# A two-layer encoder on one core: gate and up weight combinations built by accumulating DMAs, with other signs in the seven-product scheme

## The chip, the cores and the metric

One NeuronCore of a Trainium2 chip runs the whole program in one launch. The metric is the device time of that launch in microseconds (us). The engines are TensorE (PE, with its weight loads shown apart as PEld), VectorE (DVE), ScalarE (ACT), GpSimd (POOL) and SyncE (SP), which here only issues DMAs. Each engine works through its own queue in order and waits on semaphores of the others.

## The reference, cut to what matters

Two layers run over 768 tokens (512 of one request and 256 of another) with 1024 features. Each layer is a mixer (differential attention and a two-direction mLSTM), a layer norm, a feed-forward part and a second layer norm. All arithmetic is in float32. The change touches the feed-forward part and the step into it:

```python
def _conv_ffn(x, w_gu, conv_w, conv_b, w_down):
    gu = x @ w_gu                          # 1024 -> 2 * 2816
    gate, up = gu[..., :D_FF], gu[..., D_FF:]
    conv = conv_b + sum(gp[:, j:j + S] * conv_w[j] for j in range(3))   # gp: gate, padded
    hmid = jax.nn.gelu(conv) * up
    return hmid @ w_down
```

## The kernel before

**Precision.** Every matrix product is made of three passes: each float32 operand is split into a rounded part (`wh`, made by ACT) and the rest (`wl`, made by DVE), and PE adds up high by high, high by low and low by high. The splitting of one weight block of 128x512 is called a conversion here: an ACT activation (L172) and a DVE subtraction (L173).

**The gate and up products.** For each of the 22 blocks `f` of 128 hidden features, gate and up (2 outputs), the two halves of the 1024 input features and the two halves of the tokens form a two by two by two product. `ff_tile` does it with seven products of half size in the place of eight (Strassen's scheme in Winograd's form). It needs four combinations of activations (S1 to S4), made once a layer in `combine`, transposed and split in `to_strassen`, and four combinations of weights per `f`: with g0, g1 the two halves of the gate weights and u0, u1 those of the up weights, t1 = u0 - g0, t2 = u1 - t1, t3 = u1 - u0, t4 = t2 - g1. Each product is 12 matmuls of 128x384. Six PSUM banks are handed out in turn to the products (`FTAGS`).

**The weights' way.** `Weights` holds a list of pieces (DMAs of 128x512 float32, 256 KB, issued by SP into six `raw` buffers), and a list of blocks in the order in which PE takes them. Up to `NSLOT` = 12 converted blocks are held ahead of PE: when a block has been used (`done`), `pump` converts the next. A block that is a combination is built in `_value` (L150) from raw pieces just ahead of its conversion: t1 and t3 on POOL, t2 and t4 on DVE, each into one buffer of its own (tags T1 to T4). The blocks of one `f` stand in the order g0, g1, t4, t2, t3, t1, u1; for the first two (`FF_EARLY`) g0 and g1 come earlier and their first two products run ahead. The pool for the combinations (`diff_pool`) is opened in each layer at the start of the stage `wo`, in which the mixer's output projection, the residual and the first layer norm are computed in two halves of six token tiles (L881, L884, `half_stats`, `layer_norm`).

**Around it.** In the second half of `wo` each token tile goes through DVE (residual, statistics, norm), POOL (the power in `layer_norm`, L829 and L830, and `combine` for tiles 3 and 4) and then through PE transposes and ACT and DVE splits (`transposed_split`, L363 to L366). `todo` lists the five results of a tile in the order A22, S2, S3, S1, S4. The products in `ff_tile` run in the order A11, A12, A22 (p4), S2 (p6), S3 (p7), S1 (p5), S4 (p3). What DVE does with them ends in `g` (the gate, L941 and L950) and `up` (L954, L957); then come the convolution over tokens (ACT L958, DVE L960 and L961), gelu (L962), the product with up (L963) and the split of the result (L967, L968). `down(gi)` multiplies three or four such blocks with the down weights (L985, 128x512 matmuls) and adds them to the residual (L990, L992); it stands one `f` behind the group that it uses, except after the last group of a layer. The framework orders each engine's queue when the program is built, by the priorities that `prio` sets and by what it reckons to be ready.

Of the kernel before, what the change touches and what calls it, by code (L numbers as in the profile page):

```python
# [86 lines left out]
NSG = 3  # L87
AT1 = 11
# [8 lines left out]
class Weights:  # L97
# [3 lines left out]
    def __init__(self, nc, raw_pool, hl_pool, prio):  # L101
# [3 lines left out]
        self.n_dma = self.n_conv = self.n_got = self.n_done = 0  # L105
# [10 lines left out]
    def block(self, src, n, dst=None):  # L116
        self.blocks.append((src, n, dst))
        for j in self._pieces(src):
            self.uses[j] += 1
# [5 lines left out]

    def _pieces(self, src):

        if not isinstance(src, dict):
            return [src]
        if src.get("planned"):  # L130
            return []
        src["planned"] = True
        return self._pieces(src["a"]) + self._pieces(src["b"])


    def _load(self):

        while self.n_dma < len(self.dram) and (self.n_dma < NRAW or self.uses[self.n_dma - NRAW] == 0):
# [4 lines left out]
            self.n_dma += 1  # L143

    def _value(self, src, n):
        if isinstance(src, dict):
            if "tile" not in src:
                a, b = self._value(src["a"], n), self._value(src["b"], n)
                src["tile"] = self.diff_pool.tile([128, 512], F32, tag=src["tag"], name=f"{src['tag']}_{self.n_conv}")
                src["engine"].tensor_tensor(out=src["tile"], in0=a, in1=b, op=ALU.subtract)  # L150
                for x in (src["a"], src["b"]):
                    if not isinstance(x, dict):
                        self.uses[x] -= 1
            return src["tile"]
        return self.raw[src]

    def _conv(self, i):
# [16 lines left out]
        if not isinstance(src, dict):  # L174
            self.uses[src] -= 1
        self._load()

    def pump(self):

        live = sum(1 for j in range(self.n_done, self.n_conv) if self.blocks[j][2] is None)  # L180
        while self.n_conv < len(self.blocks):
            if isinstance(self.blocks[self.n_conv][0], dict) and self.diff_pool is None:
                break
# [23 lines left out]
def trunk(ctx, nc, tc, d, o, depth=DEPTH):  # L207
# [59 lines left out]
    for l in range(depth):  # L267
# [19 lines left out]
        for kind, i in ffn_seq:  # L287
            if kind == "f":

                def half(w, p):  # L290
                    return W.piece(d[w][l, i, :, p * 512:(p + 1) * 512], 512)

                if i in early:
                    g0, g1 = early[i]
                else:
                    g0, g1 = half("w_g", 0), None
                u0, u1 = half("w_u", 0), half("w_u", 1)
                if g1 is None:
                    g1 = half("w_g", 1)
                t1 = {"a": u0, "b": g0, "tag": "T1", "engine": G}  # L300
                t2 = {"a": u1, "b": t1, "tag": "T2", "engine": V}
                t3 = {"a": u1, "b": u0, "tag": "T3", "engine": G}
                t4 = {"a": t2, "b": g1, "tag": "T4", "engine": V}
                for src in (t4, t2, t3, t1, u1) if i in early else (g0, g1, t4, t2, t3, t1, u1):
                    W.block(src, 512)
# [63 lines left out]
    for l in range(depth):  # L369
# [431 lines left out]
        DF = ExitStack()  # L801
        W.diff_pool = df = DF.enter_context(tc.tile_pool(name=f"df{l}", bufs=1, reuse_waits="tile"))
# [51 lines left out]
        def combine(t):  # L854
# [73 lines left out]
        def ff_tile(f):  # L928
# [173 lines left out]
```

## Time and profile before

| | us |
|---|---|
| runs shown | 1831.13, 1832.51, 1832.93 (median 1832.51) |
| profiled execution, device time | 1831.93 |
| its span | 1830.1 |
| PE busy in the span | 1796.4 (98%) |
| DVE busy | 1345.2 (74%) |
| ACT busy | 768.2 (42%) |
| POOL busy | 241.8 (13%) |

The profile shows one execution. The span is the time from its first to its last recorded instruction; 1.8 us of the device time lie around it. The page gives busy times by engine; other views give the same by stretch of time, by line of the kernel, by wait, and as a chain of work followed back from the last instruction. A PE matmul is pipelined: one of 128x384 is shown as about 0.34 us, though one can start every 0.17 us, so the distance between starts is the time that a product costs. TensorE's granted clock is 0.999 of full speed over the span.

### The profile page before, as it was taken

How to read it: one execution, taken by the hardware profiler on the slowest of the kernel's cores; microseconds unless marked ns; L12 is line 12 of the kernel's file. 1: busy time of each engine (PE TensorE's matmuls, PEld its weight loads, DVE VectorE, ACT ScalarE, POOL GpSimd, SP SyncE). 2: the span in 40 equal slices, each digit the busy share in tenths (PEclk: the TensorE clock that was granted, in tenths of full speed). 3: DMA queues.
4: the chain of work that ended last, by engine and by line, in shares of the span. 5: the costliest groups of instructions: out<-in, count | busy, mean ns of one | idle time of the engine just before them, and what ended most of it. 6: DMA issues, size and time to landing. Idle time of an engine off the chain costs nothing.

```text
span 1830.1 us, 26254 instructions
## 1 busy us (share of the span) xinstructions
PE 1796.4 (98%) x9692; PEld 1580.8 (86%) x9692; DVE 1345.2 (74%) x2576; ACT 768.2 (42%) x1624; POOL 241.8 (13%) x260
## 2 busy tenths in 40 slices
PE   8999999999999999999999999999999999999998
PEld 8877777889899899899898777778898898898996
DVE  5546777589887787787955467785998787777878
ACT  4445567235334343243233556671443343343340
POOL 2001001141111111110110011011411111111102
PEclk9999999999999999999999999999999999999999
DMA  5312110402222122122232112113031221221211
GB/s 188 100 52 70 53 47 29 168 3 89 82 81 75 53 72 74 62 64 94 99 96 80 53 63 69 31 55 141 24 98 54 81 81 47 81 81 47 81 64 69
DMA packets 83280, 134.95 MB, mean 74 GB/s; under 512 B 7984, under 2 KB 27056, under 8 KB 83152
## 3 DMA queue, kind: packets, MB, share of 16 engines
q1 hardware_dynamic: 82432, 132.90, 22.8%
q8 instruction: 76, 1.25, 0.3%
q14 instruction: 52, 0.43, 0.1%
q10 hardware_dynamic: 720, 0.37, 0.1%
HBM read 126.86 MB, written 6.39 MB: 73 GB/s over the span
## 4 chain that ended last, share of the span: by engine, by line
PE 81%; DVE 11%; ACT 2%; POOL 2%; issue 2%; DMA 1%; SPq 0%; DVEq 0%; POOLq 0%; ACTq 0%
PE p L925 32%; PE dn L985 16%; PE wo L881 5%; PE aqkA L356 4%; PE av L346 3%; PE lo L346 3%; PE lv L346 3%; PE aqkB L356 2%; DVE wl L173 2%; PE u L727 2%; PE c1a L346 2%; PE c1b L346 2%; PE num L621 1%; PE num L617 1%; PE s L711 1%
## 5 line engine op out<-in xcount | busy, mean ns | idle before, releaser
L925 PE MATMUL p<-actA,wh 128*128 128x384 f32 x1408 | 363.4, 338 | 3.2 <-DVE g L950 3.2
L172 ACT ACTIVATE wh<-raw 128x512 fp32r<-128x512 f32 (+1 forms) x348 | 214.8, 629 | 287.5 <-PE p L925 109.1
L173 DVE TENSOR_TENSOR wl<-raw,wh 128x512 fp32r<-128x512 f32 (+1 forms) x348 | 243.4, 710 | 64.9 <-ACT wh L172 64.5
L925 PE MATMUL p<-actB,wh 128*128 128x384 f32 x1056 | 270.1, 337 | 0.0
L925 PEld LDWEIGHTS p<-actA,wh 128*128 128x128 f32 x1408 | 254.7, 188 | 5.8 <-DVE g L950 3.9
L925 PE MATMUL p<-actA,wl 128*128 128x384 f32 x704 | 237.3, 337 | 0.0
L150 POOL TENSOR_TENSOR T<-raw,raw 128x512 f32<-128x512 f32 x88 | 119.8, 1364 | 837.4 <-DVE wl L173 504.9
L985 PE MATMUL dn<-wh,actB 128*128 128x512 f32 x576 | 208.8, 396 | 1.4 <-DVE acc L992 1.4
L172 ACT ACTIVATE wh<-T 128x512 fp32r<-128x512 f32 x176 | 108.2, 628 | 220.0 <-DVE acc L992 104.9
L925 PEld LDWEIGHTS p<-actB,wh 128*128 128x128 f32 x1056 | 191.3, 188 | 0.0
L985 PE MATMUL dn<-wh,ring 128*128 128x512 f32 x480 | 179.2, 397 | 1.6 <-DVE acc L992 1.6
L925 PE MATMUL p<-actB,wl 128*128 128x384 f32 x528 | 177.2, 336 | 0.0
L992 DVE TENSOR_TENSOR acc<-acc,dn 128x512 f32<-128x512 f32 x144 | 98.2, 682 | 71.9 <-PE dn L985 71.6
L173 DVE TENSOR_TENSOR wl<-T,wh 128x512 fp32r<-128x512 f32 x176 | 129.4, 747 | 22.4 <-ACT wh L172 22.2
L985 PEld LDWEIGHTS dn<-wh,actB 128*128 128x128 f32 x576 | 108.0, 188 | 29.7 <-DVE acc L992 3.5
L925 PEld LDWEIGHTS p<-actA,wl 128*128 128x128 f32 x704 | 132.2, 188 | 0.1
L881 PE MATMUL wo<-wh,actB 128*128 128x512 f32 x384 | 122.9, 397 | 0.0
L985 PE MATMUL dn<-wl,actB 128*128 128x512 f32 x288 | 113.2, 393 | 0.0
L985 PEld LDWEIGHTS dn<-wh,ring 128*128 128x128 f32 x480 | 90.0, 188 | 24.7 <-DVE acc L992 4.2
L925 PEld LDWEIGHTS p<-actB,wl 128*128 128x128 f32 x528 | 99.1, 188 | 0.0
L985 PE MATMUL dn<-wl,ring 128*128 128x512 f32 x240 | 94.5, 394 | 0.0
L881 PEld LDWEIGHTS wo<-wh,actB 128*128 128x128 f32 x384 | 71.8, 188 | 16.2
(265 smaller groups left out, 3390.0 us busy)
## 6 DMA issues: line engine op xcount, KB each, us to landing
raw<-in_w_g_dram SPq DMA_DIRECT2D x88, 256.0 KB, 2.6
raw<-in_w_u_dram SPq DMA_DIRECT2D x88, 256.0 KB, 2.8
raw<-in_w_down_dram SPq DMA_DIRECT2D x88, 256.0 KB, 2.9
raw<-in_w_out_dram SPq DMA_DIRECT2D x32, 256.0 KB, 2.6
pt<-scr_m SPq DMA_DIRECT2D x12, 512.0 KB, 4.2
raw<-in_w_c_dram SPq DMA_DIRECT2D x16, 264.0 KB, 3.6
raw<-in_w_av_dram SPq DMA_DIRECT2D x16, 256.0 KB, 4.3
raw<-in_w_aq_dram SPq DMA_DIRECT2D x16, 256.0 KB, 3.7
```

Source lines behind the costliest of these rows:

```text
L150: src["engine"].tensor_tensor(out=src["tile"], in0=a, in1=b, op=ALU.subtract)
L172: self.nc.scalar.activation(h, v, AF.Identity)
L173: self.nc.vector.tensor_tensor(out=l, in0=v, in1=h.bitcast(F32), op=ALU.subtract)
L346: PE.matmul(ps, xh(k, t, a), (h, l)[b][:, cols], start=k + i == 0, stop=k == 7 and i == 2)
L356: PE.matmul(ps, w, actA[:, k, b, tok], start=n == 0, stop=n == 23)
L617: PE.matmul(pn[:, di * 256:di * 256 + 129], qet[r, di, hh // 2, :], cst[di, c][r, hh // 2, :], start=di == dirs[0], stop=False, skip_group ...
L621: PE.matmul(pn[:, di * 256:di * 256 + 129], pt[:, di, hh, :], vaug[:, c, hh, :], start=not dirs and di == 0, stop=di == 1, skip_group_chec ...
L727: PE.matmul(pu[:, qt * 128:(qt + 1) * 128], aT[:, st * 128:(st + 1) * 128], av[:, s0 + st, h * 128:(h + 1) * 128], start=st == 0, stop=st ...
L881: PE.matmul(p, actB[:, k, a, t * 128:(t + 1) * 128], units[k][1 + b], start=n + i == 0, stop=n == 7 and i == 2)
L925: PE.matmul(ps, blk[1 + a][:, k * 128:(k + 1) * 128], x[:, k, b, :], start=k + i == 0, stop=k == 3 and i == 2)
L985: PE.matmul(p, x, (wh_, wl_)[b], start=k + i == 0, stop=k == nf - 1 and i == 2)
L992: V.tensor_tensor(out=z, in0=z, in1=p, op=ALU.add)
```

## The change

The four weight combinations of each `f` are no longer computed by POOL and DVE. For each, SP loads a base piece from HBM into a buffer of a ring of four (`NSUM`, tag T), and POOL issues a second DMA into the same buffer that adds its source to what is there: t1 = u0 + g0, t2 = u1 + t1, t3 = u1 + u0, t4 = g1 + t2, where t1 and t2 as addends are read from their buffers in SBUF. The signs of the scheme are changed so that weights are only added: `combine` builds other signs for S1, S2 and S4 with the same number of instructions, and `ff_tile` has as many DVE operations as before. A sum is issued when its layer has begun and the sum four places earlier has been converted. The blocks of one `f` now stand in the order g0, g1, t1, t2, t3, t4, u1, and the products run in the order A11, A12, S1 (p5), S2 (p6), S3 (p7), A22 (p4), S4 (p3). u0 is no longer a raw piece, and g0 and g1 are read by DMA again for the sums.

```diff
@@ class Weights
     def block(self, src, n, dst=None):
         self.blocks.append((src, n, dst))
-        for j in self._pieces(src):
-            self.uses[j] += 1
+        if not isinstance(src, dict):
+            self.uses[src] += 1
+
+    def sum(self, base, plus):
+        s = {"base": base, "plus": plus, "read": False}
+        self.sums.append(s)
+        return s
@@ def _load(self):
+        while self.diff_pool is not None and self.n_sum < len(self.sums) and (self.n_sum < NSUM or self.sums[self.n_sum - NSUM]["read"]):
+            s = self.sums[self.n_sum]
+            if s["layer"] != self.layer:
+                break
+            s["tile"] = t = self.diff_pool.tile([128, 512], F32, tag="T", name=f"T{self.n_sum}", bufs=NSUM)
+            self.nc.sync.dma_start(t, s["base"])
+            plus = s["plus"]
+            self.nc.gpsimd.dma_start(t, plus["tile"] if isinstance(plus, dict) else plus, accum_op=ALU.add)
+            self.n_sum += 1
@@ def _value(self, src, n):
-            if "tile" not in src:
-                a, b = self._value(src["a"], n), self._value(src["b"], n)
-                src["tile"] = self.diff_pool.tile([128, 512], F32, tag=src["tag"], name=f"{src['tag']}_{self.n_conv}")
-                src["engine"].tensor_tensor(out=src["tile"], in0=a, in1=b, op=ALU.subtract)
...
@@ def trunk (the order of the blocks)
-                t1 = {"a": u0, "b": g0, "tag": "T1", "engine": G}
-                t2 = {"a": u1, "b": t1, "tag": "T2", "engine": V}
-                t3 = {"a": u1, "b": u0, "tag": "T3", "engine": G}
-                t4 = {"a": t2, "b": g1, "tag": "T4", "engine": V}
-                for src in (t4, t2, t3, t1, u1) if i in early else (g0, g1, t4, t2, t3, t1, u1):
+                u1 = W.piece(at("w_u", 1), 512)
+                t1 = W.sum(at("w_u", 0), at("w_g", 0))
+                t2 = W.sum(at("w_u", 1), t1)
+                t3 = W.sum(at("w_u", 1), at("w_u", 0))
+                t4 = W.sum(at("w_g", 1), t2)
...
+                for src in (t1, t2, t3, t4, u1) if i in early else (g0, g1, t1, t2, t3, t4, u1):
@@ def combine(t):
-            E.tensor_tensor(out=s1, in0=y0, in1=y1, op=ALU.add)
-            E.tensor_tensor(out=s2, in0=s1, in1=x0, op=ALU.subtract)
+            E.tensor_tensor(out=s1, in0=y1, in1=y0, op=ALU.subtract)
+            E.tensor_tensor(out=s2, in0=s1, in1=x0, op=ALU.add)
             E.tensor_tensor(out=s3, in0=x0, in1=y0, op=ALU.subtract)
-            E.tensor_tensor(out=s4, in0=x1, in1=s2, op=ALU.subtract)
+            E.tensor_tensor(out=s4, in0=s2, in1=x1, op=ALU.subtract)
@@ def ff_tile(f):
             V.tensor_tensor(out=g[:, lo_], in0=p2, in1=m1, op=ALU.add)
-            p4 = bank(f"p4_{f}")
-            product(p4, A22)
+            p5 = bank(f"p5_{f}")
+            product(p5, S1)
             p6 = bank(f"p6_{f}")
             product(p6, S2)
-            V.tensor_tensor(out=u2, in0=p6, in1=m1, op=ALU.add)
+            V.tensor_tensor(out=u2, in0=m1, in1=p6, op=ALU.subtract)
+            V.tensor_tensor(out=u4, in0=p5, in1=u2, op=ALU.add)
             p7 = bank(f"p7_{f}")
             product(p7, S3)
             V.tensor_tensor(out=u3, in0=p7, in1=u2, op=ALU.add)
-            V.scalar_tensor_tensor(out=g[:, hi_], in0=p4, scalar=-1.0, in1=u3, op0=ALU.mult, op1=ALU.add)
-            p5 = bank(f"p5_{f}")
-            product(p5, S1)
-            V.tensor_tensor(out=u4, in0=p5, in1=u2, op=ALU.add)
-            V.tensor_tensor(out=up[:, hi_], in0=p5, in1=u3, op=ALU.add)
+            V.scalar_tensor_tensor(out=up[:, hi_], in0=p5, scalar=-1.0, in1=u3, op0=ALU.mult, op1=ALU.subtract)
+            p4 = bank(f"p4_{f}")
+            product(p4, A22)
+            V.tensor_tensor(out=g[:, hi_], in0=p4, in1=u3, op=ALU.add)
             p3 = bank(f"p3_{f}")
             product(p3, S4)
-            V.tensor_tensor(out=up[:, lo_], in0=p3, in1=u4, op=ALU.add)
+            V.scalar_tensor_tensor(out=up[:, lo_], in0=p3, scalar=-1.0, in1=u4, op0=ALU.mult, op1=ALU.subtract)
```

## Rows read from the trace of the kernel before

**Rows 1.** The page, part 1: busy us (share) xinstructions by engine.
```profile
PE 1796.4 (98%) x9692; PEld 1580.8 (86%) x9692; DVE 1345.2 (74%) x2576; ACT 768.2 (42%) x1624; POOL 241.8 (13%) x260
```

**Rows 2.** Busy time by stretch: us, each engine's busy time (instructions), clock, DMA share, GB/s.
```profile
core 0: us, PE busy (x) PEld busy (x) DVE busy (x) ACT busy (x) POOL busy (x), PEclk, DMA share, GB/s
...
375.00:426.00 51.00, 48.63 (x276) 43.08 (x276) 47.14 (x69) 19.34 (x35) 20.88 (x20) 1.00 0.11 37
426.00:480.00 54.00, 54.00 (x283) 50.01 (x282) 51.64 (x87) 26.94 (x45) 8.56 (x6) 1.00 0.27 85
480.00:880.00 400.00, 398.40 (x2086) 371.27 (x2086) 306.97 (x501) 151.23 (x246) 42.76 (x32) 1.00 0.24 74
...
1284.00:1335.00 51.00, 48.69 (x276) 43.05 (x275) 47.12 (x69) 19.27 (x34) 20.91 (x20) 1.00 0.12 37
...
1390.00:1790.00 400.00, 398.61 (x2086) 371.52 (x2085) 305.86 (x500) 149.04 (x242) 42.43 (x32) 1.00 0.21 68
```

**Rows 3.** What PE waited for, whole span: us in total, times, longest.
```profile
PE p L925 <- DVE g L950: 3.2, 2, 1.6
PE dn L985 <- DVE acc L992: 3.0, 10, 0.5
```

**Rows 4.** The chain that ended last, 487 to 560 us: start, us, what.
```profile
487.13 43.97 PE p L925 x252
...
538.45 0.60 DVE T L150
539.05 0.61 DVE acc L992
539.66 0.04 issue
539.70 16.86 PE dn L985 x72
556.56 3.50 PE p L925 x20
```

**Rows 5.** Groups by line: the building of the combinations (busy us, mean ns, idle before).
```profile
L150 POOL TENSOR_TENSOR T<-raw,raw 128x512 f32<-128x512 f32 x88 | 119.8, 1364 | 837.4 <-DVE wl L173 504.9 <-DMA raw<-in_w_u_dram 194.0 <-DVE g L950 86.9
L150 DVE TENSOR_TENSOR T<-raw,T 128x512 f32<-128x512 f32 x44 | 32.2, 731 | 18.2 <-POOL T L150 18.2
L150 DVE TENSOR_TENSOR T<-T,raw 128x512 f32<-128x512 f32 x44 | 30.0, 682 | 0.1
```

**Rows 6.** Timeline of PE, 408 to 424 us: start, us, what, [idle before].
```profile
408.42 0.60 PE L925 MATMUL p<-actA,wh 128*128 128x384 f32 x2
...
411.39 0.52 PE L925 MATMUL p<-actB,wh 128*128 128x384 f32 x2
...
422.27 0.61 PE L925 MATMUL p<-actA,wh 128*128 128x384 f32 x2 [1.62 <-DVE g L950]
```

**Rows 7.** Timeline of DVE, 408 to 422 us.
```profile
408.60 1.87 DVE L366 TENSOR_TENSOR actB<-y0T,actB 128x512 fp32r<-128x512 f32 x3
...
411.59 0.68 DVE L150 TENSOR_TENSOR T<-raw,T 128x512 f32<-128x512 f32 x1
...
416.72 4.10 DVE L173 TENSOR_TENSOR wl<-raw,wh 128x512 fp32r<-128x512 f32 x3
420.75 0.54 DVE L949 TENSOR_TENSOR u<-p,u 128x384 f32<-128x384 f32 x1
```

**Rows 8.** Timeline of POOL in the stage wo of the first layer.
```profile
357.75 2.82 POOL L150 TENSOR_TENSOR T<-raw,raw 128x512 f32<-128x512 f32 x2 [34.47 <-DVE acc L884]
363.62 1.28 POOL L829 TENSOR_SCALAR rsa<-mva 128x1 f32<-128x1 f32 x1 [3.06 <-DVE mva L828]
...
398.45 0.19 POOL L829 TENSOR_SCALAR rsa<-mva 128x1 f32<-128x1 f32 x1
```

**Rows 9.** Timeline of all engines at the last block of the first layer.
```profile
876.58 0.55 DVE L950 SCALAR_TENSOR_TENSOR g<-p,u 128x384 f32<-128x384 f32 x1
...
882.38 0.95 DVE L963 TENSOR_TENSOR up<-up,c 128x768 f32<-128x768 f32 x1
...
884.54 0.30 PEld L985 LDWEIGHTS dn<-wh,actB 128*128 128x128 f32 x2 [0.27 <-DVE actB L968]
```

**Rows 10.** The page, part 6: DMA issues, KB each, median us to landing.
```profile
raw<-in_w_u_dram SPq DMA_DIRECT2D x88, 256.0 KB, 2.8
...
acc<-in_x_dram SPq DMA_DIRECT2D x6, 512.0 KB, 6.3
...
lng<-in_ln_g_dram SPq DMA_DIRECT2D x4, 512.0 KB, 8.6
```

More of the change, by code (lines that the diff above doesn't have):

```diff
@@ L87 @@
 NSG = 3
+NSUM = 4
 AT1 = 11
@@ L104, in __init__ @@
         self.uses, self.raw, self.hl = {}, {}, {}
-        self.n_dma = self.n_conv = self.n_got = self.n_done = 0
+        self.n_dma = self.n_conv = self.n_got = self.n_done = self.n_sum = 0
+        self.sums = []
         self.diff_pool = None
@@ L124, in unit @@
             self.block(self.piece(ap[:, c], n // 2), n // 2)
[L126 to L133, printed above, removed]
     def _load(self):
@@ L143, in _load @@
             self.n_dma += 1
+        while self.diff_pool is not None and self.n_sum < len(self.sums) and (self.n_sum < NSUM or self.sums[self.n_sum - NSUM]["read"]):
[7 more added lines that the diff above has]
+            self.n_sum += 1
     def _value(self, src, n):
         if isinstance(src, dict):
-            if "tile" not in src:
-                a, b = self._value(src["a"], n), self._value(src["b"], n)
-                src["tile"] = self.diff_pool.tile([128, 512], F32, tag=src["tag"], name=f"{src['tag']}_{self.n_conv}")
-                src["engine"].tensor_tensor(out=src["tile"], in0=a, in1=b, op=ALU.subtract)
-                for x in (src["a"], src["b"]):
-                    if not isinstance(x, dict):
-                        self.uses[x] -= 1
             return src["tile"]
@@ L173, in _conv @@
         self.nc.vector.tensor_tensor(out=l, in0=v, in1=h.bitcast(F32), op=ALU.subtract)
-        if not isinstance(src, dict):
+        if isinstance(src, dict):
+            src["read"] = True
+        else:
             self.uses[src] -= 1
@@ L181, in pump @@
         while self.n_conv < len(self.blocks):
-            if isinstance(self.blocks[self.n_conv][0], dict) and self.diff_pool is None:
-                break
+            if isinstance(self.blocks[self.n_conv][0], dict):
+                self._load()
+                if "tile" not in self.blocks[self.n_conv][0]:
+                    break
             if self.blocks[self.n_conv][2] is None:
@@ L288, in trunk, with at @@
             if kind == "f":
[L290 to L299, printed above, removed]
-                t1 = {"a": u0, "b": g0, "tag": "T1", "engine": G}
-                t2 = {"a": u1, "b": t1, "tag": "T2", "engine": V}
-                t3 = {"a": u1, "b": u0, "tag": "T3", "engine": G}
-                t4 = {"a": t2, "b": g1, "tag": "T4", "engine": V}
-                for src in (t4, t2, t3, t1, u1) if i in early else (g0, g1, t4, t2, t3, t1, u1):
+                def at(w, p):
+                    return d[w][l, i, :, p * 512:(p + 1) * 512]
+                g0, g1 = early[i] if i in early else [W.piece(at("w_g", p), 512) for p in range(2)]
+                u1 = W.piece(at("w_u", 1), 512)
[3 more added lines that the diff above has]
+                t4 = W.sum(at("w_g", 1), t2)
+                for t_ in (t1, t2, t3, t4):
+                    t_["layer"] = l
+                for src in (t1, t2, t3, t4, u1) if i in early else (g0, g1, t1, t2, t3, t4, u1):
                     W.block(src, 512)
@@ L801, in trunk @@
         DF = ExitStack()
+        W.layer = l
         W.diff_pool = df = DF.enter_context(tc.tile_pool(name=f"df{l}", bufs=1, reuse_waits="tile"))
```

## The prediction

> **What bounds the kernel now.** I read the busy times first. PE is busy for 98% of the span, DVE for 74%, POOL for 13% [rows 1]. The reader should see that the engines which the change relieves are not the one that is full. Since an average hides stages, the second view is busy time by stretch. In the two long feed-forward stretches PE works 398.4 and 398.6 of 400 us, while DVE works about 306 and POOL about 42 [rows 2]. The steps into the feed-forward part are looser: PE misses 2.4 us of 51 in the first layer and 2.3 in the second, and there DVE works 47 of 51 [rows 2]. The third view is the chain of waits, for what a feed-forward round costs: 252 matmuls of the gate and up products take 43.97 us, 0.1745 each, so a product of 12 takes 2.09 us; a round of three blocks f (487.13 to 556.56, the start of the next chain of products) takes 69.4 us, 23.1 per f [rows 4]. The fourth is the list of PE's waits: within the feed-forward part only two kinds are worth a name, a bank held until `g` is written (3.2 us in two waits, one per layer) and a bank of the down products held until DVE has added it to the residual (3.0 us in ten waits) [rows 3].
>
> From these, a ceiling for any gain: PE idle in the four kinds of stretch that the change touches is 2.4 + 2.3 (the steps) + 1.6 + 1.4 (the long stretches) = 7.7 us [rows 2]. That is 0.4% of the time, and part of it is due to transposes and splits that stay.
>
> **Work removed.** 88 POOL operations of 1364 ns and 88 DVE operations of about 707 ns go, 119.8 and 62.2 us [rows 5]. Almost all of it lies beside full PE work, so it is worth nothing by itself. It is on the path at two places. In a round, one DVE sum of 0.60 us stands in the chain directly before the addition that frees a bank for the down products [rows 4]; the ten such waits make 3.0 us [rows 3], and without the sum I take two thirds of it away: -2.0 us (bounds 0 and -3.0). At the step into the feed-forward part, the two DVE sums of the second f (the first at 411.59) and the conversions behind them, the last ones 4.1 us long, stand in DVE's queue ahead of u2 at 420.75, which `g` and then PE's wait of 1.62 us hang on [rows 6, 7]. Two sums are 1.2 us of DVE's time by the 0.60 that one costs in a chain [rows 4]. But the second f's sums can start only when the first f's buffers have been converted, so the conversions may come later in turn. I take half: -0.6 a layer, -1.2 in all (bounds 0 and -3.2, the whole of the waits).
>
> **The accumulating DMAs.** No row shows a DMA issued by POOL or one that adds. Per f there are four base loads on SP and four adding DMAs on POOL, in place of one load less (u0) and with g0 and g1 still loaded raw: 11 transfers of 256 KB instead of 4, besides the two of the down weights. That is (11 + 2) x 0.262 MB per 23.1 us, 147 GB/s, where the stretch now moves 74 at a DMA share of 0.24 [rows 2]; the share doubles and stays under half, so I cost bandwidth at nothing. What counts is the latency L of one adding DMA, from issue to landing. A plain load of this size lands after 2.8 us; loads of twice the size after 6.3 and 8.6 [rows 10]. These are the bounds; an adding DMA reads two sources of 256 KB, which puts it nearest to the 6.3, and I take 5 to 6. POOL's queue is in order: t2 waits for t1 to land, t3 is issued behind t2, t4 waits for t2, and the next t1 stands behind t4. So a round of four costs POOL two latencies plus four issues; at the 1.3 us that an operation of POOL costs here [rows 8] that is 2L + 5.2 = 17 us of the 23.1. Up to 12 blocks are converted ahead, which is 25 us of products at 2.09, so a late sum is covered. Price taken: 0. Nothing else is queued on POOL in the feed-forward part until the last group's layer norm, when all sums of the layer are long done.
>
> **Moved past in the stage wo.** The first four sums go out where POOL now builds two of the first f (357.75), and the norm of the first tile uses POOL at 363.62 [rows 8]. If t2 or t4 stands ahead of it, the norm waits for up to one L. That delays one DVE operation and its successors, while the output projection has three banks and each tile takes some 24 matmuls; I take 0. The next sums come when POOL still has the norm of the last tile to serve (398.45) [rows 8]; if an adding DMA waits there ahead of it for its base load, that is up to 2.8 us a layer [rows 10] straight on DVE's full queue. Price taken 0, bounds 0 and +5.6 for both layers.
>
> **The order of the products.** The transposed results of the last tile still come in the order A22, S2, S3, S1, S4, but the first product now needs S1 instead of A22. Today the product on A22 runs before 411.39, where the one on S2 starts [rows 6], while DVE is still splitting the last three results for actB, of which S1 is the last, until 410.47 [rows 7]. With S1 first, PE has no product for that time; it starts on S1 at about 410.5, 0.9 us earlier than it starts on S2 now, but still owes A22's 2.09: +1.2 us a layer, +2.4 in all. Bounds: 0, if the framework lets A22's product go first when it sees S1 late, and +2.1 a layer.
>
> At the end of a layer the gate's second half `g` is now written after the sixth product instead of the fifth, 2.09 us of PE later. The last f of a layer has no other f behind it, and there the chain g (876.58), convolution, gelu, product with up (882.38), split is already late by 0.27 us for PE's down products at 884.54 [rows 9]. Today u3 and a conversion stand between the fifth product's end and `g`, each about 0.6 us of DVE (as in rows of its kind, 0.54 [rows 7] and 0.60 [rows 4]); in the new order they are done before the sixth product ends, so about 1.2 of the 2.09 is made good and +0.9 a layer shows, +1.8 in all (bounds 0 and +4.2). Elsewhere a block's result is used a whole f later, at no cost. The other edits (signs in `combine`, `ff_tile`, the ring of four buffers in place of four single ones) keep the number and the shapes of the instructions: 0.
>
> **The sum.** -2.0 - 1.2 + 2.4 + 1.8 = +1.0 us on the profiled 1831.9, so 1832.9. The profiled execution lies 0.6 under the median of the runs shown: 1833.5.
>
> **A rule that speaks against the change.** In the feed-forward stretch DVE is busy for 307 of 400 us [rows 2], and POOL's two-input operations there take 1364 ns in the mean [rows 5]. The Trainium skill, "SBUF — State Buffer", section "SBUF: two separate sides", says that a DMA issued from GpSimd has its descriptors written by GpSimd's cores through a port pair that VectorE can lock them out of, so that such a DMA can take several times as long beside VectorE work. It also says that this belongs to VectorE's two-port modes, and infers that an operation of two tensors does not stop descriptors. No run so far shows either. By the rule L would grow by the wait for DVE, which is the second rival below, and I give it a small share of that chance. The same skill, "DMA: Bandwidth & Descriptors", section "Anatomy of one DMA", fits 2.0 us plus bytes over 436 GB/s, 2.6 us for 256 KB; with that L the sum stays as it is.
>
> **Rivals.** (1) DVE's relief counts in full and the new order costs nothing: -3.0 - 3.2 = -6.2, 1826. For it: both waits are DVE's, and DVE loses 62 us. Against it: S1 is the last of the three splits. Chance 0.20. (2) The sums starve PE, slower: the place is POOL's queue, the mechanism the chain t1, t2, t4 with a wait for landing twice per f, and it decides from 2L + 5.2 = 23.1, L = 9.0 us; beyond it each f costs 2(L - 9.0), so at L = 10 the 44 of them cost 88 us, 1920. For it: nothing in the trace bounds an adding DMA, and 8.6 us occurs for a transfer [rows 10]. Against it: that row has twice the bytes and a queue before it. Chance 0.08. (3) The bubbles at the two ends of the feed-forward part come at their upper bounds: 2 x (2.1 + 2.1) = 8.4, less the 2.0 of the rounds, +6.4 and 1839; an adding DMA ahead of the norm on POOL gives about as much. Chance 0.22.
>
> **Chances and range.** The forecast has 0.50. A measurement of this kernel can tell about 0.2%, 3.7 us, from no change. Faster by more: 0.19, nearly all of rival 1. Slower by more: rivals 2 and 3 and a little of the forecast, 0.33. Within: 0.48. The forecast's own range is 1829 to 1837; the range given reaches to rival 1 and beyond rival 3 with one late norm, 1825 to 1845, and leaves rival 2 out.
>
> **What would show it.** Right: PE busy stays above 398 of 400 in the long stretches; PE's wait for the residual's addition shrinks below 3.0 us; a wait of PE for a split of actB appears at the first product of each layer's feed-forward part; POOL's issues are spaced well under 23 us per four. Wrong: ACT or DVE conversions waiting for the adding DMAs for tens of us in total with PE idle behind them (rival 2), or no new wait at the step and a shorter one for `g` (rival 1).

## The result, and the profile after

The changed kernel takes 1847.08 us (median; 1846.36 to 1849.45) beside 1832.61 for the kernel before on the same chip: 1.0085 times, interval 1.0073 to 1.0098. It is slower by 14.5 us, where 1833.5 was forecast with a range up to 1845. The profiled execution after is the slowest of its four, 1849.45 us with a span of 1847.7, beside a span of 1830.1 before, so the traces have 17.6 us to explain.

The page of the changed kernel, parts 1 and 6 (busy time by engine; DMA issues with KB each and median us to landing):

```profile
PE 1801.1 (97%) x9692; PEld 1587.1 (86%) x9692; DVE 1257.9 (68%) x2488; ACT 771.2 (42%) x1624; POOL 274.5 (15%) x348
...
T<-in_w_u_dram SPq DMA_DIRECT2D x132, 256.0 KB, 3.6
...
T<-T POOLq DMA_DIRECT2D x88, 256.0 KB, 4.3
...
T<-in_w_g_dram POOLq DMA_DIRECT2D x44, 256.0 KB, 4.9
T<-in_w_u_dram POOLq DMA_DIRECT2D x44, 256.0 KB, 5.7
```

DVE has lost 87 us against [rows 1] and PE does the same 9692 matmuls. An adding DMA lands after 4.3 to 5.7 us, against 2.8 for a plain load before [rows 10].

The same stretches as in [rows 2], changed kernel (us, busy time of PE, PEld, DVE, ACT and POOL, clock, DMA share, GB/s):

```profile
375.00:426.00 51.00, 45.67 (x256) 39.20 (x254) 40.38 (x61) 19.37 (x35) 20.48 (x22) 1.00 0.33 81
426.00:480.00 54.00, 49.60 (x259) 46.91 (x260) 43.11 (x79) 25.86 (x42) 11.37 (x14) 0.97 0.76 182
480.00:880.00 400.00, 400.00 (x2090) 373.02 (x2089) 276.10 (x468) 150.14 (x244) 57.33 (x66) 1.00 0.60 148
1284.00:1335.00 51.00, 48.03 (x265) 40.83 (x265) 40.51 (x58) 16.39 (x30) 21.03 (x22) 1.00 0.21 49
1335.00:1390.00 55.00, 48.63 (x252) 47.67 (x251) 41.69 (x75) 26.48 (x45) 10.65 (x12) 0.91 0.78 191
1390.00:1790.00 400.00, 400.00 (x2078) 371.10 (x2077) 275.79 (x466) 148.58 (x241) 60.24 (x68) 1.00 0.60 147
```

The two long stretches got better: PE is busy for all of 400 us where it missed 1.6 and 1.4. The whole loss lies in the 100 us around the start of each feed-forward part. There PE is idle for 5.3 + 4.4 us in the first layer (2.4 + 0 before [rows 2]) and for 3.0 + 6.4 in the second (2.3 + 0 before), and the clock falls to 0.97 and 0.91 in the mean. The stretch from 1335 that [rows 2] leaves out, in the kernel before:

```profile
1335.00:1390.00 55.00, 55.00 (x288) 51.11 (x288) 52.13 (x89) 27.00 (x45) 8.65 (x6) 1.00 0.28 87
```

What PE waited for, whole span, changed kernel (us in total, times, longest):

```profile
PE p L929 <- DVE up L955: 12.9, 4, 4.0
...
PE y1T L366 <- DVE actA L369: 2.8, 2, 2.2
...
PE y0T L366 <- DVE actA L369: 1.9, 2, 1.4
...
PE dn L989 <- DVE acc L994: 0.9, 1, 0.9
```

The two kinds of wait in [rows 3] are gone (the wait for `g`) or down from 3.0 to 0.9 (the down products). A new kind stands in their place, four waits of 12.9 us in all: a PSUM bank held until DVE has written the second half of `up` (L955). All four fall in the start of a feed-forward part. Here they are in the timeline of PE (start, us, what, idle before):

```profile
426.84 0.62 PE L929 MATMUL p<-actB,wh 128*128 128x384 f32 x2 [3.99 <-DVE up L955]
...
459.00 0.62 PE L929 MATMUL p<-actA,wh 128*128 128x384 f32 x2 [2.52 <-DVE up L955]
...
1343.42 1.01 PE L929 MATMUL p<-actB,wh 128*128 128x384 f32 x2 [3.88 <-DVE up L955]
...
1376.12 0.66 PE L929 MATMUL p<-actA,wh 128*128 128x384 f32 x2 [2.49 <-DVE up L955]
```

**Why `up` is late.** Timelines of POOL, ACT and DVE ahead of the first of these waits, changed kernel (`wh` is ACT's half of a conversion, `wl` DVE's, and T is a buffer of the ring):

```profile
419.33 0.88 POOL L150 DMA_DIRECT2D T<-in_w_g_dram  x1 [2.20 <-ACT wh L173]
...
403.41 0.64 ACT L173 ACTIVATE wh<-T 128x512 fp32r<-128x512 f32 x1 [2.79 <-DMA T<-in_w_g_dram]
...
424.96 0.63 ACT L173 ACTIVATE wh<-T 128x512 fp32r<-128x512 f32 x1 [2.43 <-DMA T<-in_w_g_dram]
...
413.87 1.28 DVE L174 TENSOR_TENSOR wl<-T,wh 128x512 fp32r<-128x512 f32 x2
...
418.71 0.69 DVE L174 TENSOR_TENSOR wl<-T,wh 128x512 fp32r<-128x512 f32 x1 [3.09 <-ACT wh L173]
...
423.42 0.55 DVE L954 TENSOR_TENSOR u<-p,u 128x384 f32<-128x384 f32 x1
425.62 0.69 DVE L174 TENSOR_TENSOR wl<-T,wh 128x512 fp32r<-128x512 f32 x1 [1.65 <-ACT wh L173]
426.23 0.55 DVE L955 SCALAR_TENSOR_TENSOR up<-p,u 128x384 f32<-128x384 f32 x1
```

Read it from the end. `up` at 426.23 needs only p5 and the u3 that DVE wrote at 423.42; it could have run at about 424. But DVE's queue is in order, and ahead of `up` stands the conversion of the first sum of the third f, at 425.62. That waits for ACT's half of the conversion at 424.96, which has waited 2.43 us for the adding DMA. POOL issued that DMA at 419.33 into the ring buffer that had held the second f's t1. ACT had converted that t1 at 403.41, but DVE did its half only at 413.87, after the splits of the last tile and the first f's blocks. SP's base load into the buffer followed at 414.62 and landed at 418.64 by the trace's semaphores. (The view puts POOL's wait of 2.20 us down to an ACT conversion, which ended at about that time but doesn't use this buffer.) So the ring of four had no free buffer until DVE had converted the second f's sums. PE needs none of this block yet. It needs the bank that `up` frees.

The third f's sum explains only the last 2.3 us of the delay. u3 was late already. The product that it needs was done when PE went on to the next one at 418.35, but DVE had waited 3.09 us for the second f's third sum before 418.71, and had that conversion, u2, u4 and four more conversions to do until 423.42.

The waits at 459.00 and 1376.12 are the echo of the same thing, through ACT. ACT and DVE before 459.00, changed kernel:

```profile
443.61 0.64 ACT L173 ACTIVATE wh<-T 128x512 fp32r<-128x512 f32 x1 [3.33 <-DMA T<-T]
445.81 0.63 ACT L173 ACTIVATE wh<-T 128x512 fp32r<-128x512 f32 x1 [1.56 <-DMA T<-in_w_u_dram]
449.22 0.63 ACT L173 ACTIVATE wh<-T 128x512 fp32r<-128x512 f32 x1 [2.77 <-DMA T<-T]
449.76 1.02 ACT L962 ACTIVATE c<-g,convw 128x768 f32<-128x768 f32 x1
...
450.81 1.15 DVE L964 SCALAR_TENSOR_TENSOR c<-g,convw,c 128x255 f32<-128x255 f32 x2 [3.64 <-ACT c L962]
```

ACT stands still for 7.7 us in three waits for sums. Behind them in its queue are the convolution at 449.76 and the copy `m`; DVE waits 3.64 us for the convolution and then has no gap until it reaches `up` at 458.39.

**The clock.** Stretches of 2 us after the second layer's first wait for `up` and after its second one, changed kernel, columns as above:

```profile
1344.00:1346.00 2.00, 2.00 (x8) 2.00 (x7) 0.30 (x1) 0.17 (x1) 0.00 (x0) 0.50 0.81 121
1346.00:1348.00 2.00, 2.00 (x8) 2.00 (x7) 1.27 (x3) 1.39 (x2) 0.87 (x1) 0.50 0.91 164
...
1376.00:1378.00 2.00, 1.88 (x7) 1.88 (x8) 2.00 (x5) 0.77 (x1) 0.00 (x0) 0.64 1.12 204
1378.00:1380.00 2.00, 2.00 (x8) 2.00 (x7) 2.00 (x5) 1.67 (x4) 0.20 (x1) 0.51 1.04 303
1380.00:1382.00 2.00, 2.00 (x13) 2.00 (x13) 2.00 (x4) 0.34 (x1) 0.68 (x1) 1.00 0.91 274
```

The granted clock is 0.50 there, TensorE's level of 1.2 GHz, and 8 matmuls fall in 2 us where 13 do at 1.00. The time lost, (1 - clock) summed over the time in which PE works, is 1.7 us after the wait at 426.84 (clock 0.91, 0.50, 0.74 in the stretches of 2 us from 426 to 432), 2.9 after the one at 1343.42 and 1.7 after the one at 1376.12: 6.3 us. After the wait at 459.00 the clock stayed at 1.00.

**The sum of the two traces.** New waits for `up` +12.9; clock +6.3; transposes of the last tile waiting for the splits of actA 4.7 instead of 1.1, +3.6; the waits for `g` gone, -3.2; the waits of the down products -2.1. That is +17.5 of 17.6. A wait at the start of the program (c1a, 8.0 us after 7.2 before) moved by 0.8 without having to do with the change, so the agreement is good to about 1 us.

The transposes belong to the same cause in part. ACT stands before the second f's t2, and the split for which a transpose waits stands behind it:

```profile
407.26 0.63 ACT L173 ACTIVATE wh<-T 128x512 fp32r<-128x512 f32 x1 [2.73 <-DMA T<-T]
...
409.16 0.66 PE L366 MATMUL y0T<-ident,S 128*128 128x128 f32 x4 [1.37 <-DVE actA L369]
```

### The profile page after: what moved, and what is told of

It is laid out like the page before. It is cut to its first block, busy times and chain, and to the rows that moved or that the text cites. A ratio compares the mean times of both kernels' runs of the same rounds, so it can differ in the third digit from the quotient of the medians.

```text
span 1847.7 us, 26847 instructions
## 1 busy us (share of the span) xinstructions
PE 1801.1 (97%) x9692; PEld 1587.1 (86%) x9692; DVE 1257.9 (68%) x2488; ACT 771.2 (42%) x1624; POOL 274.5 (15%) x348
## 5 line engine op out<-in xcount | busy, mean ns | idle before, releaser
L174 DVE TENSOR_TENSOR wl<-raw,wh 128x512 fp32r<-128x512 f32 (+1 forms) x348 | 236.9, 691 | 80.5 <-ACT wh L173 80.0
L929 PE MATMUL p<-actB,wh 128*128 128x384 f32 x1056 | 274.8, 341 | 8.2 <-DVE up L955 7.9
L174 DVE TENSOR_TENSOR wl<-T,wh 128x512 fp32r<-128x512 f32 x176 | 123.1, 704 | 58.3 <-ACT wh L173 57.9
L150 POOL DMA_DIRECT2D T<-T x88 | 77.2, 878 | 322.8 <-issue 69.0
L150 POOL DMA_DIRECT2D T<-in_w_g_dram x44 | 38.9, 885 | 451.1 <-DMA T<-in_w_u_dram 231.6
```

Source lines behind the costliest of these rows:

```text
L150: self.nc.gpsimd.dma_start(t, plus["tile"] if isinstance(plus, dict) else plus, accum_op=ALU.add)
L174: self.nc.vector.tensor_tensor(out=l, in0=v, in1=h.bitcast(F32), op=ALU.subtract)
L929: PE.matmul(ps, blk[1 + a][:, k * 128:(k + 1) * 128], x[:, k, b, :], start=k + i == 0, stop=k == 3 and i == 2)
```

## The experiments

**Theories.** D: the time is lost at the start of each feed-forward part alone, because conversions of late sums stand in in-order queues (DVE's, in its narrow form) ahead of the operations that free banks. Its rivals: the new order of products and blocks costs it; the new signs cost it; the sums come too slowly at any depth of the ring (rate), against too late because they are issued too late (depth). All medians below stand beside runs of the kernel before on the same chip; these had medians of 1831.2 to 1831.8. The changed kernel's own difference is +14.5 us.

In several runs some f are taken back to POOL and DVE additions (t1 and t3 on POOL, t2 and t4 on DVE, from raw pieces), with the new signs and the new order; ENG says which f. The core of that edit:

```diff
-                t1 = W.sum(at("w_u", 0), at("w_g", 0))
-                t2 = W.sum(at("w_u", 1), t1)
+                if i in ENG:
+                    t1 = W.sum(u0, g0, G)
+                    t2 = W.sum(u1, t1, V)
+                    ...
@@ def _value(self, src, n)
+                src["engine"].tensor_tensor(out=src["tile"], in0=a, in1=b, op=ALU.add)
```

### Which part of the change costs the time

**old_order**: engine sums for all f, and the blocks and products in the order of the kernel before; of the change only the signs stay.

```diff
+ENG = range(NFF)
-                for src in (t1, t2, t3, t4, u1) if i in early else (g0, g1, t1, t2, t3, t4, u1):
+                for src in (t4, t2, t3, t1, u1) if i in early else (g0, g1, t4, t2, t3, t1, u1):
@@ def ff_tile(f): products A22, S2, S3, S1, S4
```

> New signs, but all sums by POOL and DVE and the old order of blocks (t4, t2, t3, t1) and products (A22, S2, S3, S1, S4). Theory: the signs cost nothing, 1830 to 1834, so the 8 us by which the kernel with all sums on the engines and the new order (1839.7) lies above the kernel before are the new order's. Rival: the signs or the ring cost it, 1838 or above.

Measured 1832.28 us, 0.9999 [0.999, 1.0008]. Its waits are those of [rows 3] (for `g` 3.2 us in 2, for the down products 2.8 in 10). The signs cost nothing.

**eng_all**: engine sums for all f, new order.

```diff
+ENG = range(NFF)
```

> All four combinations of every f are added by POOL (t1, t3) and DVE (t2, t4) from raw pieces, as before the change, while signs, block order and product order stay the new ones; no DMA adds. Theory D (late sums at the start of the feed-forward part hold DVE's in-order queue, so banks are freed late): the four waits of PE for up L955, 12.9 us in the changed kernel, fall under 4 us, and the time is 1831 to 1835. Rival O (the new order of products costs it): the time stays at 1842 or above.

Measured 1839.71 us, 1.0043 [1.0029, 1.0058], +8.1 on its kernel before. PE's waits, eng_all:

```profile
PE dn L1014 <- DVE acc L1021: 6.8, 10, 0.8
...
PE p L954 <- ACT m L966: 2.3, 2, 1.1
PE dn L1014 <- DVE acc L1019: 1.9, 2, 0.9
```

No wait for `up` without adding DMAs, as D says; the time is above D's 1835 and below the 1842 of rival O, because the new order by itself costs 7.6 us beside old_order (8.1 - 0.4), and most of that in the rounds: the down products now wait for 8.7 us in 12 where they waited 3.0 in 10.

**eng_0to3**: engine sums for f = 0 to 3 only, adding DMAs from f = 4 on.

```diff
+ENG = (0, 1, 2, 3)
```

> Only the combinations of f = 0 to 3 of each layer are added by POOL and DVE; from f = 4 on the DMAs add. Theory D: the late sums are only those of the start, so the four waits of PE for up go and the shorter waits in the rounds stay: 1827 to 1833. Rival B (adding DMAs cost in every f, through latency or traffic): most of the 14.5 us remains, 1840 or above, since 18 of 22 f still use them.

Measured 1828.74 us, 0.9984 [0.9975, 0.9994]: 2.9 us below the kernel before, and the fastest of all kernels here. PE's waits, eng_0to3:

```profile
PE p L954 <- ACT m L966: 2.2, 2, 1.1
...
PE y0T L391 <- DVE actA L394: 1.0, 2, 0.6
PE y1T L391 <- DVE actA L394: 1.0, 2, 0.6
PE dn L1014 <- DVE acc L1019: 0.9, 2, 0.8
```

The waits for `up` are gone, the clock is back at 0.999 in the mean, and PE works 400.00 of 400 us in both long stretches. So adding DMAs in f = 4 to 21 cost nothing, and all of the loss comes from the first four f of a layer. Beside eng_all they are worth 11.0 us (8.1 + 2.9), of which 7.8 are waits of the down products (8.7 to 0.9).

**dma_0to3**: the opposite half, adding DMAs for f = 0 to 3 and engine sums behind.

```diff
+ENG = range(4, NFF)
```

> The complement of the run with engines for f = 0 to 3: DMAs add for f = 0 to 3 of each layer, POOL and DVE from f = 4 on, in the new order. Theory D: the four waits of PE for up L955 are back with 10 us or more, and the relief in the rounds is gone, so this is the slowest of the mixes: 1850 to 1860. Rival B: only 8 of 44 f use adding DMAs, so the time is near that of all sums on the engines, 1838 to 1843.

Measured 1870.37 us, 1.0212 [1.0195, 1.0229], +38.5; D's number was 10 to 20 us too low. The waits for `up` are there again (9.6 us in 4), as D says. But its price and that of the order (14.5 and 8.1) don't add up to 38.5. PE's waits, dma_0to3:

```profile
PE dn L1014 <- DVE acc L1019: 12.0, 2, 6.0
PE p L954 <- DVE up L980: 9.6, 4, 3.8
...
PE dn L1014 <- DVE acc L1021: 6.5, 10, 0.8
```

The two waits of 6.0 us are new, one per layer, at the first down products (in the first layer until 479.14). From 462.5 to the addition at 478.41 that frees their bank, DVE has one gap, of 0.56 us, and three sums of 0.68 us stand in that stretch: the late start runs straight into the engine sums. These are 2.0 of the 6.0 us; that the rest is what the late start left undone is argued, and no run takes it apart. Against eng_all the waits listed for PE in the feed-forward parts and the transposes are 18.7 us longer, and the clock, which is 0.50 after four of its waits and never below 1.00 during PE's work in eng_all, costs 8.9 us by the sum used above. That is 27.6, where the two spans differ by 29.0.

### What at the start: which f, whose queue, rate or depth

**eng_1** and **eng_12**: engine sums only for f = 1, and only for f = 1 and 2.

```diff
+ENG = (1,)        # eng_1
+ENG = (1, 2)      # eng_12
```

> Only the sums of f = 1 of each layer are added by POOL and DVE; those of f = 0 (built early, in the stage wo) and from f = 2 on come by DMA. Theory D: the sums of f = 1 were late because they wait for the conversion of f = 0 at the end of wo; the late ones now are f = 2's, with a whole f more of products ahead of them, so most of the 12.9 us of waits go: 1829 to 1836. If the DMAs need several f to catch up: 1838 to 1847.

> As the run with engines for f = 0 to 3 (1828.7), but engines only for f = 1 and 2. Theory D: f = 0's sums are built in the stage wo in either case, and by f = 3 the conversions run ahead of PE: 1827 to 1831. If the catching up takes until f = 3: 1832 to 1840.

Measured 1844.45 us, 1.0067 [1.0052, 1.0082], and 1833.51 us, 1.0007 [0.9998, 1.0017] (its ten runs spread from 1830.2 to 1836.5). D's ranges failed in both, and the other ones held: relief for f = 1 alone regains 1.5 of the 14.5 us, and the wait is now for `g` (9.6 us in 2, the first ending at 430.37). Two f regain 12.4, four regain 17.4. The delay isn't one gap that closes once it is bridged: with the ring of four the sums keep coming about as slowly as PE uses them. That they get ahead when the first down products give them time fits these runs, but no run shows it by itself.

**wl_pool**: the low halves of all blocks that are sums go to POOL, so that DVE doesn't stand before a late sum.

```diff
-        self.nc.vector.tensor_tensor(out=l, in0=v, in1=h.bitcast(F32), op=ALU.subtract)
+        (self.nc.gpsimd if isinstance(src, dict) else self.nc.vector).tensor_tensor(out=l, ...)
```

> As the changed kernel, but the low part of each combined block (L174) is subtracted on POOL instead of DVE; the sums are as late as before. Theory D: DVE has nothing in its queue that waits for a sum, PE's waits for up L955 fall from 12.9 to under 3 us and the time is 1830 to 1837. Rival S (PE lacks the late weights themselves): the waits of PE only change their name, to the low part on POOL, and the time is 1843 or above.

Measured 1881.37 us, 1.0271 [1.0254, 1.0288]. This says little on D: the 176 subtractions take 1523 ns each on POOL, 258 us in all, and stand in the queue that issues the adding DMAs; PE waits 14.3 us for the down products in 16 waits and 10.0 for `combine` on POOL. What it shows is that this queue has no room for other work.

**wl_pool_1to3**: the same for f = 1 to 3 alone.

```diff
+        (self.nc.gpsimd if isinstance(src, dict) and src["f"] in (1, 2, 3) else self.nc.vector)...
```

> As the changed kernel, all sums by DMA, but the low parts of the combined blocks of f = 1, 2 and 3 alone are subtracted on POOL instead of DVE; this doesn't load POOL in the other 19 f. Theory D: in the start DVE no longer stands behind late sums, PE's waits for up L955 go from 12.9 to under 4 us: 1832 to 1840. Rival S (PE lacks the late weights): the waits come back under another name, 1845 or above. POOL's own queue then holds the next sums behind these subtractions, which may cost some of the gain.

Measured 1849.62 us, 1.0099 [1.0084, 1.0114], no gain. PE's waits, wl_pool_1to3:

```profile
PE p L929 <- DVE up L955: 7.9, 4, 2.9
...
PE p L929 <- DVE g L945: 7.0, 2, 3.6
```

The waits for `up` shrink from 12.9 to 7.9, and as much comes back as waits for `g`. D's narrow form, DVE's queue alone, falls: ACT stands before the same late sums with its own half of each conversion, and behind that are the raw conversions, the copy `m` and the convolution which DVE's operations need (as at 449.22 above). It is the whole in-order stream of conversions on both engines.

**nsum5, nsum6_raw5, nsum7_raw4, raw4**: deeper rings, which let sums be issued earlier. To make room, six and seven buffers were paid for with raw ones; raw4 is the control, four raw buffers with the ring of four.

```diff
-NSUM = 4
+NSUM = 5      # nsum5; 6 with NRAW = 5, 7 with NRAW = 4 in the other two
```

> The ring of sums has five buffers instead of four. Theory D: each sum of the start can be issued one converted block earlier, some 2 to 4 us, so the four waits shrink by about that, from 12.9 in all to 2 to 8 us: 1836 to 1843. Rival O or B: no change, 1846 to 1849.

> All sums by DMA, the ring of sums with six buffers, and five raw buffers instead of six to make room. If the sums of the start are late because they are issued late (a buffer must be converted first): one more buffer takes a further 3 us or more off the run with five (1843.5): 1834 to 1841. If the rate at which POOL's chain makes sums is the limit (some 14.4 us for the four of one f, as fast as PE uses them): no further gain, 1842 to 1848.

> All sums by DMA, seven sum buffers and four raw buffers. Issued late: 1829 to 1837, plus what four raw buffers cost by the run beside it. Rate: 1842 to 1848, plus the same.

> The changed kernel with four raw buffers instead of six and the ring of four as it is: what the room taken from the raw pieces costs by itself. Between 0 and +10 on 1847.1 by either theory.

| ring, raw buffers | median us | ratio | over its kernel before |
|---|---|---|---|
| 4, 6 (the change) | 1847.08 | 1.0085 [1.0073, 1.0098] | +14.5 |
| 5, 6 | 1843.5 | 1.0062 [1.0047, 1.0077] | +11.8 |
| 6, 5 | 1838.05 | 1.0037 [1.0023, 1.005] | +6.9 |
| 7, 4 | 1837.61 | 1.0033 [1.0021, 1.0044] | +6.4 |
| 4, 4 (raw4) | 1850.07 | 1.0103 [1.0085, 1.012] | +18.9 |

Depth helps from four to five (just clear of the noise) and to six. In nsum5 the waits for `up` are gone and 10.3 us in two waits for `g` stand in their place, so it lies 0.5 us above D's range. From six to seven the time stays the same within the noise, but with one raw buffer less, and raw buffers may cost time of themselves (raw4 is 4.4 us worse than the change, with overlapping intervals; if that is real and adds up, the ring of seven is at +2.0). Timeline of POOL, nsum7_raw4, the first adding DMAs of the third, the fourth and the sixth f:

```profile
400.97 0.90 POOL L150 DMA_DIRECT2D T<-in_w_g_dram  x1
...
418.88 0.90 POOL L150 DMA_DIRECT2D T<-in_w_g_dram  x1
...
445.83 1.12 POOL L150 DMA_DIRECT2D T<-in_w_g_dram  x1
```

The first two are issued 18.4 and 14.9 us earlier than in the change (419.33 and 433.76). The sums are late because they are issued late, and they are issued late because a buffer must be converted first. The rate isn't fixed either: the sixth f's DMA at 445.83 follows the fifth's (433.83) after 12.0 us, where four buffers give 14.4 to 14.8. So a fixed rate, the other reading, falls. What remains in nsum7_raw4 is 7.1 us of waits at the same place (for `m` 5.6, for `g` 1.5), so a ring of seven with four raw buffers doesn't cure it. Seven buffers beside all six raw ones weren't tried.

### What the new order costs

**eng_all_ge** and **g_early**: the product on A22 and its block t4 one place earlier, ahead of S3, so that `g` needs no more than before; with engine sums for all f, and for f = 0 to 3.

```diff
-                for src in (t1, t2, t3, t4, u1) if i in early else (g0, g1, t1, t2, t3, t4, u1):
+                for src in (t1, t2, t4, t3, u1) if i in early else (g0, g1, t1, t2, t4, t3, u1):
@@ def ff_tile(f): products S1, S2, A22, S3, S4
```

> All sums on POOL and DVE, as in the run that gave 1839.7, but with A22 as the fifth product (S1, S2, A22, S3, S4), so that g is written as early as in the kernel before. If the late g is what the new order costs (8 us over the run with the old order, 1832.3): PE's waits of the down products for the residual's addition fall from 8.7 to about 3 us and the time is 1831 to 1835. If it is something else in the order (the order of the sums): 1838 or above.

> As the run with engines for f = 0 to 3 and DMAs from f = 4 on (1828.7), but A22 is the fifth product again (S1, S2, A22, S3, S4) and t4 is converted ahead of t3, so that g is written after the fifth product and not the sixth. If the late g is what the new order costs: 1822 to 1827. If that cost is gone once DVE has no sums to add: 1827 to 1831.

Measured 1833.89 us, 1.0015 [1.0005, 1.0024], and 1834.88 us, 1.0014 [1.0005, 1.0023]. With engine sums, the earlier A22 gives back 5.6 of the 7.6 us that the order costs (+8.1 to +2.4). With the sums of f = 4 and later made by DMA it gives nothing: g_early is 5.9 us worse than eng_0to3 (+3.0 against -2.9), above both ranges. The loss in g_early is the old mechanism again. Timelines of ACT and DVE, g_early:

```profile
464.19 0.63 ACT L187 ACTIVATE wh<-T 128x512 fp32r<-128x512 f32 x1 [5.58 <-DMA T<-T]
...
464.86 0.69 DVE L188 TENSOR_TENSOR wl<-T,wh 128x512 fp32r<-128x512 f32 x1 [3.94 <-ACT wh L187]
465.46 0.55 DVE L982 TENSOR_TENSOR g<-p,u 128x384 f32<-128x384 f32 x1
465.93 0.55 DVE L983 SCALAR_TENSOR_TENSOR up<-p,u 128x384 f32<-128x384 f32 x1
```

A conversion waits 3.94 us, and `g` and `up` stand behind it; the first down products wait 6.3 us in all. The sum is t4 of the fifth f, the first f whose sums come by DMA. The edit moved t4 ahead of t3 among the blocks and the engine sums, but the DMAs still go out in the order t1, t2, t3, t4, so this one was issued last, at 457.62. What an earlier A22 gives with t4's DMA moved too wasn't run. Little is left to gain: in eng_0to3, with the late `g`, the down products wait 0.9 us in all, against 8.7 in eng_all. So the late `g` costs much only while DVE also makes sums.

**eng_0to3_todo**: eng_0to3 with the results of the last tile transposed in the order in which the products need them, S1 first.

```diff
-            todo[t] = [(A22, y1), (S2, s2), (S3, s3), (S1, s1), (S4, s4)]
+            todo[t] = [(S1, s1), (S2, s2), (S3, s3), (A22, y1), (S4, s4)]
```

> As the run with engines for f = 0 to 3 (1828.7), but the results of a tile are transposed in the order in which the products take them (S1, S2, S3, A22, S4). If S1 coming fourth costs as the prediction says, 1.2 us a layer: 1825 to 1827.5. If the framework hides it: 1828 to 1830.

Measured 1830.66 us, 0.9993 [0.9984, 1.0002], no better than 0.9984 [0.9975, 0.9994]. Its profiled execution has a new wait of 2.0 us at the first down products and a clock of 0.50 behind it, so the median alone doesn't settle it. The place itself does: in the 51 us from 375 PE works 48.58 us here, 48.65 in eng_0to3 and 48.63 in the kernel before [rows 2]. That S1 comes fourth costs nothing there.

## Why the prediction was wrong, point by point

**The step that failed** is the price of 0 for the adding DMAs. It stood on two sentences: a round of four costs POOL 17 of the 23.1 us that PE takes for an f, and "Up to 12 blocks are converted ahead, which is 25 us of products at 2.09, so a late sum is covered". Both describe the steady rounds, and there they hold (PE 400.00 of 400). At the start neither does.

- The demand: the first f of a layer follow each other without down products between them. Seven products of 2.09 us are 14.6 us per f, not 23.1. The first adding DMAs of the third, fourth and fifth f go out at 419.33, 433.76 and 448.57, so the supply of 14.4 to 14.8 us per f just keeps up and can't catch up. The ring sets this pace: t1's buffer is free for the next f's t1 only when t2, which reads it, has landed (SP's base loads waited 17.4 us in 4 for such landings from 375 to 480). From 414.62 the base load, t1 and t2 land one after the other, and the next base load goes out at 429.05. It fits that one f of relief (eng_1) regained so little.
- The cover: the sums of the second f can only start when those of the first are converted, with a ring of four. The prediction said so in the sentence on the -1.2 us, and used it there to halve a gain. It should have been carried to the next paragraph: no block made from a sum is ahead at that time. The deeper rings show this term by itself, 1847.1 to 1837.6 us.
- The queues: for POOL the prediction asked what stands behind a waiting instruction ("Nothing else is queued on POOL"). For ACT and DVE it didn't ask, though their conversions wait for the same DMAs, and the operations which free PE's banks stand behind them. The last paragraph of the prediction named this sign, "conversions waiting for the adding DMAs", but tied it to rival 2 and L above 9 us.

The term was 0 and came out as +12.9 for the waits, about +6 for the clock behind them, and +2.7 of the +3.6 at the transposes: there eng_all, which makes no sums by DMA, waits 2.0 us, the change 4.7.

Of the four signs of being right that the prediction names, three came out: PE above 398 of 400, 0.9 us for the residual's addition, 14.4 to 14.8 us per four issues. The fourth, a wait for a split of actB at the first product, came to 0.3 us in both layers together. None of them looks at what the first f wait for, so they can't tell this loss from no loss.

**L was about right**: 5 to 6 us taken, medians 4.3 (half of them), 4.9 and 5.7 measured, none above 7.7. The Trainium skill, "DMA: Bandwidth & Descriptors", section "Anatomy of one DMA", gives 2.6 us for 256 KB by its fit; here the measurement decides. The same skill, "SBUF — State Buffer", section "SBUF: two separate sides", has the lock-out of such DMAs by VectorE that was weighed as a rule against this change. No run here shows landings that are several times longer: the longest is 7.7 us here and 8.9 in any run, and POOL's issues take 0.86 to 1.19 us beside a DVE that is busy for 276 of 400 us. Whether a part of the 1.7 to 3.1 us by which the medians lie above 2.6 comes from it stays open. So rival 2 was right about starved conversions and wrong about what starves them.

**Bandwidth**: the rate of 147 GB/s was right (148 and 147). The DMA share was not: it went from 0.24 to 0.60, more than double, and to above 1.0 in the stretches around the first wait (422 to 428). The landing of the sum issued at 419.33, about 5.6 us, is 0.7 above the median, and its base load took 4.0, where a load of this size took 2.8 before [rows 10]. So up to about 2 us of that chain may be the traffic's; no run takes it apart.

**The rounds**: -2.0 us for the down products' waits were forecast, and the waits fell by 2.1. What was not seen is how much the new order leans on this: with DVE still making sums the order costs 7.6 us (eng_all), of which the late `g` is 5.6. The prediction looked for the late `g` only at the last f of a layer (+1.8), where no wait appeared, and said "Elsewhere a block's result is used a whole f later, at no cost". That holds only with the sums off DVE.

**The step**: the wait for `g` did vanish, -3.2 instead of -1.2, but into a longer one. Without late sums neither shows in the sum: in the first layer's step PE works 48.65 of 51 us in eng_0to3 and 48.63 before, and a wait for `m` (1.1 us) stands where the one for `g` stood. The +2.4 for S1 coming fourth is 0 by eng_0to3_todo. **Signs** 0 (old_order), right. **The norm on POOL** in `wo`, 0: the first one starts at 364.59 after 363.62 [rows 8], and waits for DVE, not for an adding DMA; right. At the last tile an adding DMA does stand ahead of the norm (399.29, the norm at 400.26), but its base load had landed, so it costs POOL the 0.90 us of an issue; eng_all has an addition of 1.27 us in that place.

**The rivals**: rival 1, relief in full, has its sum of -6.2 and needs a start without late sums; eng_0to3 comes nearest, at -2.9. Rival 3 put the loss at the two ends of the feed-forward part and came nearer in size (1839) than the forecast, but by bubbles that didn't occur: that is luck.

**Open**: how the 14.5 us divide exactly between waits and clock in the median execution, since only the slowest of the four was profiled; whether a ring of seven with six raw buffers would do without eng_0to3's engine sums, and what each in-order queue, ACT's and DVE's, costs by itself, since no run relieves ACT's.

## What to carry to other kernels

A steady rate says nothing of the start: work out supply and demand again for the first rounds, where the consumer runs at its fastest and nothing has been made ahead. When work moves from an engine to a DMA, list for each engine that waits for the landing what is queued behind that wait, and whether a PSUM bank or a buffer is freed there. Then move only the part that has cover: here the first four f stay on the engines, the other eighteen go to DMAs, and the kernel is faster than both versions (1828.74 us, 0.9984 [0.9975, 0.9994]).

## What the runs showed of the hardware that was not expected

- After three of four idle times of PE, 3.99, 3.88 and 2.49 us long, the granted clock was at 0.50 for some 3.4 to 6.8 us; after one of 2.52 us it stayed at 1.00. In eng_0to3_todo it fell after one of 1.99 us (0.50 in the stretch from 470 to 472). So two stalls of the same length may cost differently, and the price of a stall was up to 1.75 times its length (3.88 + 2.9 us). The Trainium skill, "TensorE: Matmul & The Clock Gate", section "Why this matters for your kernels", tells the reader to avoid longer idle gaps between matmuls because the clock falls in them. The trace agrees at 3.99 and 3.88 us; near 2.5 us and below it this case shows both.
- An adding DMA from SBUF to SBUF lands earlier (4.3 us) than one from HBM (4.9 and 5.7), and a plain load of 256 KB into the same ring takes 3.6 beside them, after 2.8 before the change [rows 10].
- POOL's additions of two tensors took 1524 ns each in eng_all, after 1364 for the subtractions before [rows 5].
